# Shifting the start of the resident moving operands within their slots, by 16 to 256 bytes

## The chip, the cores and the metric

The kernel runs on one core of a Trainium2 chip. The metric is the device time of one execution, in microseconds. A profiled execution gives the trace; other executions are only timed.

## What is computed

One layer of a streaming encoder, on a prompt of 4096 rows and a sample of 32 rows, each row 1024 wide, in float32. The parts that matter here:

```
h = rmsnorm(x, norm_g)
proj = jnp.einsum('btd,de->bte', h, w_in)
u, v, z_a, xb, z_b = jnp.split(proj, [W_A, 2 * W_A, 3 * W_A, 3 * W_A + W_B], axis=-1)
v_n = layernorm(v, ln_v_g, ln_v_b)
a = u * chunk_mlp(v_n, w_spatial, b_spatial) * jax.nn.silu(z_a)
...
b = pool_mix(x_ext, pos0, w_pool, pool_scale) * jax.nn.silu(z_b)
y = x + jnp.einsum('bte,ed->btd', jnp.concatenate([a, b], axis=-1), w_out)
...
y_prompt = rmsnorm(xp, final_g)
```

`chunk_mlp` mixes the 128 positions of a chunk by a matrix per head; `pool_mix` takes trailing means of 2, 4, 8 or 16 rows, followed by a linear map per group of channels. Also returned are the last 15 rows of the pooling branch and the normalised v of the sample.

## The kernel before

**Products.** Each large product of two matrices is cut into 2 x 2 blocks and done with seven block products instead of eight (the operands are sums and differences of blocks, `q` from 0 to 6). Every float32 operand is split into a high and a low part of type float32r; a block product takes three terms (high x high, high x low, low x high) for each of four slices of the contraction: twelve matmuls, in `product` (line 186, the matmul is line 193) and in `OutPair.product` (line 708, matmuls on lines 712 to 714). A matmul has a stationary operand of 128 x 128 and a moving operand of 128 partitions by 512 columns in most places.

**Slots.** `slot()` (line 105) hands out one of seven buffers, one for each `q`, of 2 * 4 * 528 float32 (16896 bytes, 33 x 512) in each of the 128 partitions. In the program's memory layout they follow one another from byte 18432 (36 x 512) of a partition, so each begins at a multiple of 512 bytes. A slot holds a moving operand for a whole stage, while stationary operands (`weight_tile`, line 624, tiles named wop, also at multiples of 512 bytes) pass by. The stages:

- A first phase (lines 211 to 613) turns the normalised rows into operands and computes v, the slots holding v's weights (`wv`, line 264). It stores the operands of the rows in memory (`xops`, `xops_l`).
- Four blocks of 1024 rows each (`Tokens`, line 915). The slots hold the rows' operands, and the sixteen column sets of the input projection (`Set`, line 938: eight of kind gate, eight of kind pool) pass as stationary. Block 0's slots are filled by `load_first` (line 589): six of seven get two quarters by DMA and two by a VectorE and a ScalarE copy (lines 599, 600), the seventh comes by DMA alone. Blocks 1 and 2 are filled by `Tokens.load` (line 922, DMAs on line 931), block 3 by its other branch (line 926).
- The output projection in two halves z = 0 and 1 of the contraction. Here the slots hold operands made of `w_out`, loaded by `load_out_weights` (line 632, DMA on line 634), and the rows pass as stationary in sixteen pairs of 128 rows (`OutPair`, line 657; `LastPair`, line 746, is the last of all, and does its last product in two parts of 256 columns). Two small sample products use the same slots (`OutSample`, lines 843 to 845).

**Where a matmul starts in its slot.** `Tokens.moving` (line 933) gives it. In blocks 0 to 2 a slot is laid out as (half h, quarter j, slice k, 128 columns), and a matmul reads for one h and k the four quarters: four runs of 512 bytes, 2048 bytes apart, starting at h x 8192 + k x 512 bytes. In block 3, whose halves carry 16 sample rows each, the layout is (h, k, 528 columns), and a block product is done as two groups of 264 columns: one run of 1056 bytes, starting at h x 8448 + k x 2112 bytes, plus 1056 for the second group. The output weights are laid out as (k, h, 512 columns): one run of 2048 bytes.

**Order.** The order of the products is written out in lists (lines 1078 to 1091). At a change of stage two sets or pairs a and b run lagged: (a,0), (a,1), (b,0), (a,2), (b,1), (a,3), (b,2), (a,4), (a,5), (b,3), (a,6), (b,4), (b,5), (b,6). After b's product q the slot q is free, and its next contents are loaded by SP's queue (lines 1165 to 1171, 1266 and 1267). The next stage begins in the same lagged order, so its seventh slot is wanted ten products after the stage's first. On SP's queue the loads of the weights of the next sets and of the rows stand between the slot loads. While gate sets run, four spatial matmuls (line 998) stand between products at two places of each set.

Of the kernel before, what the change touches and what calls it, by code (L numbers as in the profile page):

```python
# [9 lines left out]
F32R = mybir.dt.float32r  # L10
# [5 lines left out]
P = 128  # L16
D = 1024
# [8 lines left out]
NB = 4  # L26
# [3 lines left out]
WIDE = HALF + EXT  # L30
TOT = SEQ + DEC
NQ = 7
WARM = 14


@with_exitstack
def stream_step(ctx: ExitStack, tc, x_prompt, x_sample, state_pool, norm_g, w_in, ln_v_g, ln_v_b,
# [18 lines left out]
    slots = ctx.enter_context(tc.tile_pool(name="slots", bufs=NQ))  # L56
# [45 lines left out]
        return y, guess + 3 * [lambda: stt(t, y, y, m, ALU.mult, ALU.mult),  # L102
                               lambda: stt(y, t, 1.5, y, ALU.add, ALU.mult)]

    def slot():
        return slots.tile([P, 2 * 4 * WIDE], F32R, tag="slot", name="slot")


    behind = []
# [101 lines left out]
    with ExitStack() as ph:  # L211
# [23 lines left out]
        def tr_tile():  # L235
            return ps_tr.tile([P, 512], F32, tag="tr", name="tr")

        g_bc = g_p.tile([P, D], F32, name="g_bc")
        first_ops = {}
# [9 lines left out]
        warm = tr_tile()  # L249
        for _ in range(WARM):  # L250
            tc.keep_in_program_order(nc.tensor.transpose(warm[:, :P], ident, ident))
# [10 lines left out]


        wv = [slot()[:, :8 * HALF].rearrange("p (h k n) -> p h k n", h=2, n=HALF) for _ in range(NQ)]

        v_raws = {}
# [87 lines left out]
        class Past:  # L354


            def load(self):
                self.st = half(), half()
                for z in range(2):
                    nc.gpsimd.memset(self.st[z][:HALO], 0.0)  # L360
                    nc.sync.dma_start(self.st[z][1:HALO], state_pool[0, 0, :, z * 512:(z + 1) * 512])
# [226 lines left out]

        def load_first(q):

            first_ops[q] = t = slot()
            dst = t[:, :8 * HALF].rearrange("p (h j x) -> p h j x", h=2, j=4)
            src = xops[0].rearrange("j p (q h x) -> q h p j x", q=NQ, h=2)
            n = 2 if q < NQ - 1 else 4
            for h in range(2):
                nc.sync.dma_start(dst[:, h, :n].bitcast(F32), src[q, h, :, :n])
            if n == 4:
                return
            nc.vector.tensor_copy(dst[:, :, pa.j], pa.ops[q])
            nc.scalar.copy(dst[:, :, pb.j], pb.ops[q])  # L600
# [4 lines left out]
        for n, (pair, q) in enumerate(lagged(pa, pb)):  # L605
            for step in {0: steps[:2], 1: steps[2:3], 2: steps[3:4], 4: steps[4:5], 6: steps[5:6], 7: steps[6:]}.get(n, []):
                step()
            if n == 1:
                norms([], [(v, P) for v in pairs[-3].v])
                pairs[-3].store()  # L610
            pair.product(q)
            if pair is pb:
                load_first(q)
# [16 lines left out]
    w_slots = {}  # L630

    def load_out_weights(z, q):
        w_slots[z, q] = t = slot()[:, :4 * D].rearrange("p (k h n) -> p k h n", k=4, h=2)
        nc.sync.dma_start(t.bitcast(F32), wops[z, q].rearrange("p k (h n) -> p k h n", h=2))

    class OutWeights:
# [227 lines left out]
    with ExitStack() as ph:  # L864
# [50 lines left out]
        class Tokens:  # L915
# [4 lines left out]
                self.groups = [(0, HALF)] if not self.last else [(0, WIDE // 2), (WIDE // 2, WIDE // 2)]  # L920

            def load(self, q):
                t = slot()
                self.ops[q] = t
                if self.last:
                    nc.sync.dma_start(t.bitcast(F32), xops_l[q].rearrange("p x t -> p (x t)"))
                    return
                src = xops[self.b].rearrange("j p (q h x) -> q h p j x", q=NQ, h=2)
                for h in range(2):
                    dst = t[:, h * 4 * HALF:(h + 1) * 4 * HALF].rearrange("p (j x) -> p j x", j=4)  # L930
                    nc.sync.dma_start(dst.bitcast(F32), src[q, h])
# [214 lines left out]
        for n in range(n_sets):  # L1146
# [9 lines left out]
            for s, q in order:  # L1156
                at += 1
                prepare(at + LEAD)
                while later:
                    (later.pop(0) or (lambda: None))()  # L1160
                for c, c0, w in cs[id(s)]:
                    s.product(c, q, c0, w)
                if n == 0 and q == 0:
                    behind.append(s)
                if s is g[-1] and groups[n + 1][0].stage != s.stage:
                    if n + 1 < n_sets:
                        groups[n + 1][0].tok.load(q)
                    else:
                        if q == 3:
                            groups[n_sets][1].begin([raw_tile(), raw_tile()], True)  # L1170
                        load_out_weights(0, q)
                if n == 0 and s is g[-1] and q in (3, 5):
                    next(constants, None)
                if s.kind == "gate" and q in (2, 4):
                    if q == 2:
                        s.t1 = []
                    s.t1.append(s.spatial(len(s.t1)))
                if s.kind == "gate" and q == 6 and s.tok.last:
                    s.spatial_sample()
                if q == NQ - 1:  # L1180
                    later.append(s.finish_gate() if s.kind == "gate" else s.finish_pool())
# [4 lines left out]
    with ExitStack() as ph:  # L1186
# [56 lines left out]
        for n in range(n_sets, len(groups)):  # L1243
# [6 lines left out]
            for m, (s, q) in enumerate(order):  # L1250
                at += 1
                prepare(at + LEAD)
                if m == 0 and n in samples:
                    samples[n].load()
                k = n - n_sets - 4
                if k == KT and m == 2:
                    sample_rows()
                if 0 <= k < KT and m in (0, 2):
                    state_load(k) if m == 0 else state_split()
                s.multiply(q)  # L1260
                if n == n_sets and s is g[0] and q == NQ - 1:
                    s.finish()
                if m == 2 and ended:
                    for x in ended:
                        x.finish()
                if s is g[-1] and n + 1 < len(groups) and groups[n + 1][0].stage != s.stage:
                    load_out_weights(1, q)
                if 0 <= k < KT and m == 6:
                    state_rows(k)
# [34 lines left out]
```

## Time and profile before

| | us |
|---|---|
| median of 2 runs | 2347.69 (2346.55 to 2348.82) |
| span of the profiled execution | 2345.9 |
| TensorE busy | 2328.8 |
| VectorE busy | 1790.2 |
| ScalarE busy | 896.4 |
| GpSimd busy | 215.1 |

The span runs from the first to the last instruction of one profiled execution; the timed runs count a little around it. Busy time of an engine is the time in which it has an instruction under way. "PE" is TensorE's matmuls, "PEld" its weight loads, which run beside them; a matmul's busy time contains its latency, so neighbours overlap, and the distance from start to start is what one costs in a row of many.

### The profile page before, as it was taken

Reading aid. Unit: us, or ns where it says so; the run is one execution under the profiler, and the core shown is the slowest. Engines: PE = TensorE matmul, PEld = TensorE weight load, DVE = VectorE, ACT = ScalarE, POOL = GpSimd, SP = SyncE. Lnnn points to the kernel's source line nnn. Section 1 sums busy time; section 2 is a strip of 40 time slices with the busy share of each in tenths; the row PEclk is TensorE's granted clock in tenths of the full one; section 3 lists DMA queues with packets and bytes.
Section 4 is the critical chain, followed back from the end, with each engine's and each line's share of the span. In section 5 each row is a group of like instructions: output and inputs, shape, how many; then the busy total and the mean of one; then the engine's idle time right before and its main releaser. Section 6 shows DMA issues by size and latency. Waiting matters only on the chain.

```text
span 2345.9 us, 32604 instructions
## 1 busy us (share of the span) xinstructions
PE 2328.8 (99%) x11936; PEld 1981.3 (84%) x11936; DVE 1790.2 (76%) x3318; ACT 896.4 (38%) x1603; POOL 215.1 (9%) x398
## 2 busy tenths in 40 slices
PE   8999999999999999999999999999999999999998
PEld 7878888888888888888888899999987878888877
DVE  7877786866787767877668876668777778688887
ACT  6545544433433333433334333334322333233333
POOL 1010000100021000111000110102200000000000
PEclk9999999999999999999999999999999999999999
DMA  8879977432448334483334472335587776955542
GB/s 309 316 241 279 275 255 245 142 104 89 149 144 296 99 100 134 135 300 122 108 108 148 177 262 87 101 100 164 223 294 265 252 257 232 360 171 169 159 137 90
DMA packets 325145, 445.69 MB, mean 190 GB/s; under 512 B 19324, under 2 KB 248444, under 8 KB 322296
## 3 DMA queue, kind: packets, MB, share of 16 engines
q1 hardware_dynamic: 273384, 355.05, 45.9%
q0 software_dynamic: 22288, 73.48, 8.3%
q10 hardware_dynamic: 29312, 15.08, 2.4%
q8 instruction: 94, 1.54, 0.3%
q14 instruction: 67, 0.55, 0.1%
HBM read 273.88 MB, written 169.66 MB: 189 GB/s over the span
## 4 chain that ended last, share of the span: by engine, by line
PE 95%; DMA 2%; DVE 2%; issue 0%; ACT 0%; SPq 0%; ACTq 0%; DVEq 0%
PE acc L193 66%; PE acc L712 8%; PE acc L713 8%; PE acc L714 8%; PE sp L998 2%; PE tr L473 1%; DMA wops<-raw 1%; DMA vt<-in_w_in_dram 1%; PE acc L261 0%; DMA op<-in_w_in_dram 0%; PE more L844 0%; PE more L843 0%; DVE wop L81 0%; DVE y L724 0%; PE acc L202 0%
## 5 line engine op out<-in xcount | busy, mean ns | idle before, releaser
L193 PE MATMUL acc<-slot,wop 128*128 128x512 f32 (+1 forms) x6720 | 1260.9, 348 | 1.0 <-DVE wop L81 1.0
L193 PEld LDWEIGHTS acc<-slot,wop 128*128 128x128 f32 x6720 | 1081.1, 188 | 156.5 <-DVE wop L81 1.4
L81 DVE TENSOR_TENSOR wop<-raw,wop 128x512 fp32r<-128x512 f32 (+1 forms) x510 | 353.4, 695 | 133.0 <-ACT wop L119 121.7
L119 ACT CAST wop<-raw 128x512 fp32r<-128x512 f32 x340 | 210.5, 622 | 384.4 <-PE acc L193 266.9
L712 PE MATMUL acc<-slot,wop 128*128 128x512 f32 x892 | 347.2, 389 | 1.5 <-DVE y L724 1.5
L713 PE MATMUL acc<-slot,wop 128*128 128x512 f32 x892 | 347.1, 389 | 0.0
L714 PE MATMUL acc<-slot,wop 128*128 128x512 f32 x892 | 347.0, 389 | 0.0
L193 PE MATMUL acc<-slot,op 128*128 128x512 f32 x1344 | 323.8, 395 | 0.3 <-ACT vt L167 0.2
L193 PEld LDWEIGHTS acc<-slot,op 128*128 128x128 f32 x1344 | 247.6, 188 | 51.9 <-ACT vt L167 0.7
L165 DVE TENSOR_TENSOR t<-acc,t 128x512 f32<-128x512 f32 (+1 forms) x320 | 186.7, 584 | 120.0 <-ACT t L174 65.5
L724 DVE TENSOR_TENSOR y<-acc,y 128x512 f32<-128x512 f32 x235 | 159.3, 687 | 72.6 <-PE acc L714 72.2
L712 PEld LDWEIGHTS acc<-slot,wop 128*128 128x128 f32 x892 | 167.4, 188 | 37.8 <-ACT wop L677 2.3
L714 PEld LDWEIGHTS acc<-slot,wop 128*128 128x128 f32 x892 | 167.4, 188 | 34.8
L713 PEld LDWEIGHTS acc<-slot,wop 128*128 128x128 f32 x892 | 167.4, 188 | 34.7
L677 ACT CAST wop<-raw 128x512 fp32r<-128x512 f32 x160 | 98.7, 622 | 175.2 <-PE acc L714 164.9
L81 DVE TENSOR_TENSOR wop<-sum,wop 128x512 fp32r<-128x512 f32 x200 | 136.9, 685 | 25.7 <-ACT wop L119 24.9
L1017 POOL DMA_DIRECT2D abT<-t x128 | 69.2, 541 | 843.2 <-DVE t L1029 622.7
L119 ACT CAST wop<-sum 128x512 fp32r<-128x512 f32 x136 | 84.5, 622 | 96.9 <-PE acc L193 72.0
L1040 DVE TENSOR_TENSOR t<-t 128x527 f32<-128x527 f32 (+3 forms) x160 | 111.1, 698 | 0.6
L677 ACT CAST wop<-sum 128x512 fp32r<-128x512 f32 x64 | 39.7, 622 | 119.5 <-PE acc L714 96.3
L174 ACT COPY t<-acc 128x512 f32<-128x512 f32 (+1 forms) x80 | 40.2, 504 | 107.1 <-PE acc L193 105.4
L115 DVE TENSOR_TENSOR sum<-raw 128x512 f32<-128x512 f32 x68 | 46.8, 688 | 44.7 <-DMA raw<-in_w_in_dram 44.1
(236 smaller groups left out, 1955.0 us busy)
## 6 DMA issues: line engine op xcount, KB each, us to landing
raw<-in_w_in_dram SPq DMA_DIRECT2D x102, 512.0 KB, 4.3
xops<-op SPq DMA_DIRECT2D x72, 512.0 KB, 6.1
abT<-t POOLq DMA_DIRECT2D x128, 256.0 KB, 3.8
raw<-abT SPq DMA_DIRECT2D x64, 512.0 KB, 5.0
slot<-xops SPq DMA_DIRECT2D x30, 1024.0 KB, 9.6
slot<-wops SPq DMA_DIRECT2D x14, 2048.0 KB, 9.7
xt<-in_x_prompt_dram SPq DMA_DIRECT2D x32, 512.0 KB, 5.0
raw<-v_all SPq DMA_DIRECT2D x32, 512.0 KB, 3.3
```

What stands on the lines that cost most here:

```text
L81: return nc.vector.tensor_tensor(out, src, hi.bitcast(F32), ALU.subtract)
L119: pair = nc.scalar.copy(hi, src), lo_part(lo, src, hi)
L165: add = lambda o, x, y: nc.vector.tensor_tensor(o, x, y, ALU.add)
L193: mm(acc, stationary(s, k), moving(m, k), start=fresh and n == 0, stop=n == len(terms) - 1, skip_group_check=True)
L677: nc.scalar.copy(t[:, 0], src)
L712: mm(acc, x[:, 0, k, :], w[:, k, 0, c], start=fresh and k == 0, stop=False, skip_group_check=True)
L713: mm(acc, x[:, 0, k, :], w[:, k, 1, c], start=False, stop=False, skip_group_check=True)
L714: mm(acc, x[:, 1, k, :], w[:, k, 0, c], start=False, stop=k == 3, skip_group_check=True)
L724: nc.vector.tensor_tensor(y, self.acc[bank], y, ALU.add)
L998: mm(sp[:, a, :], self.v[:, 4 * hf + a, :], WT[:, h, :], start=True, stop=True)
L1017: nc.gpsimd.dma_start(abT[row, :, t0:t0 + HALF], t[:, :HALF])
L1040: tt(nxt[:, lo:HALO + m], s[:, lo:HALO + m], s[:, lo - step:HALO + m - step], ALU.add)
```

## The change

A slot's contents begin a given number of float32 past the slot's start: 8 (32 bytes) in block 0, 16 (64) in block 1, 32 (128) in block 2, none in block 3, 64 (256) for z = 0 and 4 (16) for z = 1 of the output projection. The buffers keep their size and place; the views into them, written by the loads and copies and read by the matmuls, are the same behind the shift. The 4096 float32 used and at most 64 in front fit into 4224. The first phase's `wv` calls `slot()` without a shift.

```diff
@@ -31,6 +31,7 @@
 TOT = SEQ + DEC
 NQ = 7
 WARM = 14
+SHIFT = (8, 16, 32, 0, 64, 4)
@@ -102,8 +103,9 @@
-    def slot():
-        return slots.tile([P, 2 * 4 * WIDE], F32R, tag="slot", name="slot")
+    def slot(shift=0):
+        t = slots.tile([P, 2 * 4 * WIDE], F32R, tag="slot", name="slot")
+        return t[:, shift:] if shift else t
@@ -588,7 +590,7 @@
         def load_first(q):
 
-            first_ops[q] = t = slot()
+            first_ops[q] = t = slot(SHIFT[0])
@@ -630,7 +632,7 @@
     def load_out_weights(z, q):
-        w_slots[z, q] = t = slot()[:, :4 * D].rearrange("p (k h n) -> p k h n", k=4, h=2)
+        w_slots[z, q] = t = slot(SHIFT[NB + z])[:, :4 * D].rearrange("p (k h n) -> p k h n", k=4, h=2)
         nc.sync.dma_start(t.bitcast(F32), wops[z, q].rearrange("p k (h n) -> p k h n", h=2))
@@ -920,7 +922,7 @@
             def load(self, q):
-                t = slot()
+                t = slot(SHIFT[self.b])
                 self.ops[q] = t
```

## The prediction

> **What bounds the kernel now.** I read the page first (busy time, slices, chain), then the chain of waits cut to single stages, then the timeline of the last output pair, then the DMA views.
>
> ```profile
> span 2345.9 us, 32604 instructions
> PE 2328.8 (99%) x11936; PEld 1981.3 (84%) x11936; DVE 1790.2 (76%) x3318; ACT 896.4 (38%) x1603; POOL 215.1 (9%) x398
> PEclk9999999999999999999999999999999999999999
> PE acc L193 66%; PE acc L712 8%; PE acc L713 8%; PE acc L714 8%; PE sp L998 2%; PE tr L473 1%; DMA wops<-raw 1%; DMA vt<-in_w_in_dram 1%; PE acc L261 0%; DMA op<-in_w_in_dram 0%; PE more L844 0%; PE more L843 0%; DVE wop L81 0%; DVE y L724 0%; PE acc L202 0%
> ```
>
> TensorE is busy 99% of the span at full granted clock, and the chain that sets the end is 66% line 193 plus three times 8% for lines 712 to 714: the products whose moving operand lies in the slots. So whatever these matmuls gain or lose each goes into the time in full, and what the other engines do goes in only if it arrives late. The matmuls that the change reaches:
>
> ```profile
> L193 PE MATMUL acc<-slot,wop 128*128 128x512 f32 x4032 | 928.1, 390 | 1.0 <-DVE wop L81 1.0
> L712 PE MATMUL acc<-slot,wop 128*128 128x512 f32 x892 | 347.2, 389 | 1.5 <-DVE y L724 1.5
> L713 PE MATMUL acc<-slot,wop 128*128 128x512 f32 x892 | 347.1, 389 | 0.0
> L714 PE MATMUL acc<-slot,wop 128*128 128x512 f32 x892 | 347.0, 389 | 0.0
> L193 PE MATMUL acc<-slot,wop 128*128 128x264 f32 x2688 | 332.9, 285 | 0.0
> L844 PE MATMUL more<-slot,wop 128*32 128x512 f32 x32 | 12.0, 394 | 0.0
> L843 PE MATMUL more<-slot,wop 128*64 128x512 f32 x28 | 10.9, 391 | 0.0
> L845 PE MATMUL more<-slot,wop 128*64 128x512 f32 x4 | 1.6, 394 | 0.0
> L713 PE MATMUL more<-slot,wop 128*128 128x256 f32 x8 | 2.3, 283 | 0.0
> ```
>
> Columns: count, then busy time and mean of one, then idle time before them. Shifted are the 4032 of blocks 0 to 2 (1344 each) and, in the output projection, 3 x 892 = 2676, the 64 sample matmuls (32 + 28 + 4) and 3 x 8 = 24 narrow ones: 2764. Together 6796. The 2688 with 264 columns are block 3, shift 0, untouched. The mean of one (390 ns) is latency of a pipelined instruction; the price is the spacing, which the chain gives as length of a piece by its count, and the windows give by stage:
>
> ```profile
> 397.08:720.64 323.56, 322.61 (x1487) 1.00 0.45 147
> 720.64:1039.84 319.20, 319.20 (x1474) 1.00 0.46 154
> 1039.84:1359.04 319.20, 319.20 (x1474) 1.00 0.46 154
> 1359.04:1704.40 345.36, 345.36 (x2834) 1.00 0.44 152
> 767.09 0.89 PE sp L998 x8
> 774.33 13.62 PE acc L193 x60
> 1409.61 5.83 PE acc L193 x48
> 1422.17 0.33 PE sp L1009 x2
> 1422.50 8.94 PE acc L193 x72
> 2324.68 0.39 PE L714 MATMUL acc<-slot,wop 128*128 128x512 f32 x1
> ...
> 2334.88 0.39 PE L714 MATMUL acc<-slot,wop 128*128 128x512 f32 x1
> 2335.11 0.28 PE L712 MATMUL more<-slot,wop 128*128 128x256 f32 x1
> ...
> 2337.86 0.28 PE L714 MATMUL more<-slot,wop 128*128 128x256 f32 x1
> ```
>
> The four windows are blocks 0 to 3, each from its first matmul to the first of the next stage (window, its length, TensorE busy); then pieces of the chain (start, length, count); then the timeline. Block 1: 16 spatial pieces (8 gate sets, two halves) of 0.89 us are 14.24; (319.20 - 14.24) / 1344 = 226.9 ns a matmul, and 13.62 / 60 = 227.0 agrees. Output projection: 45 steps from 2324.68 to 2334.88 are 226.7 ns for 512 columns; 23 steps from 2335.11 to 2337.86 are 119.6 ns for 256 columns. So a column costs (226.7 - 119.6) / 256 = 0.418 ns, and 226.7 - 512 x 0.418 = 12.5 ns are fixed per matmul. All of these start on multiples of 512 bytes.
>
> **The change, part by part.** Nothing is added or removed: same instructions, same sizes, same buffers and waits; only the start of slot contents moves.
>
> (1) The moving reads. Block 3 is the row of before that reads off the 512-byte grid: there a matmul starts at h x 8448 + k x 2112 + (0 or 1056) bytes into a slot, so at every multiple of 64, and for the second column group 32 past one. (345.36 - 14.24 - 8 x 0.33) / 2688 = 122.2 ns. The aligned rows give 12.5 + 264 x 0.418 = 122.9 ns. Off the grid costs nothing there. Ends: the chain's pieces of block 3 run from 5.83 / 48 = 121.5 ns (1.4 under the line) to 8.94 / 72 = 124.2 ns (1.3 over). I take 0, because the whole block is nearest to it; carried to 6796 matmuls the ends are -9.5 and +8.8 us. What block 3 does not show: a 16-byte start, and runs of 512 bytes that lie across the grid (its run is 1056 bytes in one piece). In blocks 0 to 2 a matmul reads four runs of 512 bytes, 2048 apart; the output weights are one run of 2048. Four runs cost 226.9, one 226.7: 0.2 / 3 = 0.07 ns for starting another run while all lie on the grid.
>
> The nearest rows therefore set the price of a start at under 0.1 ns, but aligned. [...]
>
> (2) The loads of the slots, issued by SP, write to shifted places.
>
> ```profile
> L931 SPq DMA_DIRECT2D slot<-xops x28: 359/500/3952, 690.9 to 1041.4; - x28
> DMA to landing us min/median/max: 5.6/9.6/15.9
> L634 SPq DMA_DIRECT2D slot<-wops x14: 319/330/457, 1672.6 to 2026.0; - x14
> DMA to landing us min/median/max: 8.5/9.7/15.5
> L596 SPq DMA_DIRECT2D slot<-xops x14: 359/420/934, 367.4 to 397.7; - x14
> DMA to landing us min/median/max: 3.8/5.4/12.5
> raw<-in_w_out_dram SPq DMA_DIRECT2D x8, 512.0 KB, 3.7
> spare<-in_w_out_dram SPq DMA_DIRECT2D x8, 512.0 KB, 4.8
> ```
>
> Each line of a load is followed by its time from issue to landing. Cover: the last L931 issue, 1041.4, is block 2's seventh slot. In the lagged order its first product is the eleventh of the block; the block starts at 1039.84, a product is 12 x 0.227 = 2.72 us, so it is wanted at 1067.0. At the longest landing it is there at 1057.3: 9.7 us spare. Likewise for the output weights: last issue 2026.0 + 15.5 = 2041.5, wanted ten products after the stage begins, which is when the last load is issued (it follows the old stage's last product in the program): 2026.0 + 27.2 = 2053, 11 us spare. Block 0: 397.7 + 12.5 = 410.2, wanted ten products after 397.08, at 424: 14 spare. The price: in the program's memory layout the spare tiles lie 480 bytes past a multiple of 512 and the raw tiles on one; the same source and size lands in 4.8 against 3.7 us, a factor of 1.3 at most from alignment. 15.9 x 1.3 = 20.7: 1062.1, before 1067.0. So 0, and the cover is gone at a factor of (1067.0 - 1041.4) / 15.9 = 1.61. Behind a slower load on SP's queue wait the raw loads of the next sets, which lead their use by several products too.
>
> [...]
>
> (3) Block 0's slots are partly written by copies on VectorE and ScalarE.
>
> ```profile
> L599 DVE CAST slot<-op x6: 684/690/694, 367.4 to 395.5; 128x1024 fp32r<-128x1024 f32 x6
> L600 ACT CAST slot<-op x6: 1049/1056/1062, 369.0 to 394.6; 128x1024 fp32r<-128x1024 f32 x6
> ```
>
> If the shifted target took VectorE's faster rate away, the nearest bound is ScalarE's rate for the same shape: 6 x (1.056 - 0.690) = 2.2 us of VectorE, spread over 28 us and with the same 14 us of cover as the loads beside them. If it got faster, nothing waits for it. So 0; uncovered, at most +2.2.
>
> Sum: 0 + 0 + 0. Profiled span 2345.9, median of the runs 2347.69, so 1.8 us lie around the span: 2347.7, say **2348**. The likeliest case's own range is 2348 - 9.5 - 0 to 2348 + 8.8 + 0: 2338 to 2357.
>
> **Rivals.** (B) Straddling runs stall the read (slower). Place: lines 193 and 712 to 714. Every 512-byte run that is off the grid touches one piece of SBUF more: 4 x 4032 + 2764 = 18892 starts. Price between 0.07 ns (the row above: +1.3 us) and a whole new stream, 12.5 ns: +236 us, 2584. It decides the sign past 2% (47 us) from 47 / 18892 = 2.5 ns a start. Where pieces are 64 bytes, only block 0 (5376) and the second output half (1382) pay: 6758 x 12.5 = 84 us, 2432. For it: no row has such runs. Against: block 3's 1056 bytes are not a whole number of 64-, 128- or 512-byte pieces, and its spacing still lies on the straight line by columns, so part pieces are free at least at the end of a run.
>
> (C) The fixed 12.5 ns come from the moving and stationary reads both beginning on the same grid (the wop tiles lie on multiples of 512), and the shift parts them (faster). All gone: 6796 x 12.5 = 85 us, 2263; over 2% from 6.9 ns. Against: in block 3 the two starts differ by 32 to 480 bytes in most matmuls, and 122.2 - 264 x 0.418 = 11.8 ns are still there.
>
> (D) The loads become late. Twice as long, block 2's last slot lands at 1041.4 + 31.8 = 1073.2, 6.2 us late; block 1 the same; each output half 2026.0 + 31.0 - 2053 = 4 us: about 21 us, 2369. For it: the 1.3 above; against: it needs 1.61 before anything shows.
>
> **How the numbers follow.** Forecast A (nothing moves) 0.76; B 0.13, of which 0.02 below 2.5 ns a start; C 0.07, of which 0.06 over 2%; D 0.04. The predicted time is A's. A alone holds 2338 to 2357. To leave out no more than 2 in 10 the range reaches up to D and the cheap end of B, 2372, and down to 2337. A measurement of this kernel can tell about 2% from no change, so: faster 0.06, same 0.76 + 0.02 + 0.01 + 0.04 = 0.83, slower 0.11.
>
> **What would show it.** A: blocks 0, 1, 2 again 323.6, 319.2 and 319.2 us long, output spacing 226.7 ns in both halves. B: longer blocks, each by its own shift: block 0 alone and the second output half with small pieces, all five stages with 512-byte ones; single matmuls spaced wider, no idle time. C: the shifted stages under 220 ns a matmul while block 3 stays at 122. D: spacing unchanged, TensorE idle before the first products of blocks 1 and 2 with a DMA into a slot as releaser. The forecast is wrong if any stage's spacing moves by over 1.5 ns, or if idle time appears at a stage's start.

## The result, and the profile after

| | us |
|---|---|
| before, median of 2 runs | 2347.69 (2346.55 to 2348.82) |
| after, median of 2 runs | 2374.94 (2374.70 to 2375.19) |
| ratio after / before | 1.0115 (1.0094 to 1.0135) |
| span of the profiled execution, before and after | 2345.9 and 2372.9 |

The change costs 27 us, 1.15%. Timed again beside two of the experiments on one chip it cost the same: 1.0111 (1.0096 to 1.0126).

The page of the kernel after, span, engines and granted clock:

```profile
span 2372.9 us, 32604 instructions
PE 2354.6 (99%) x11936; PEld 1981.4 (84%) x11936; DVE 1794.9 (76%) x3318; ACT 897.1 (38%) x1603; POOL 206.9 (9%) x398
PEclk9999999999999999999999999999999999999999
```

The same instructions, the same clock, TensorE busy 99% of a longer span: the time did not go into waiting. The windows of the kernel after, each from a stage's first matmul to the next stage's (blocks 0, 1, 2, 3, output halves 0 and 1; the last ends at the first of the 24 narrow matmuls):

```profile
396.25:728.24 331.99, 331.15 (x1487) 1.00 0.44 144
728.24:1050.39 322.15, 322.15 (x1474) 1.00 0.46 152
1050.39:1377.87 327.48, 327.48 (x1474) 1.00 0.45 152
1377.87:1722.82 344.95, 344.95 (x2833) 1.00 0.44 151
1722.82:2046.26 323.44, 319.96 (x1410) 1.00 0.78 270
2046.26:2362.23 315.97, 315.97 (x1366) 1.00 0.47 159
```

The prediction showed blocks 0 to 3 of the kernel before. The output halves of the kernel before, in the same view:

```profile
1704.24:2025.78 321.54, 320.02 (x1410) 1.00 0.79 272
2025.78:2335.11 309.33, 309.33 (x1365) 1.00 0.49 162
```

Stage by stage the difference is +8.4 us (shift 32), +2.9 (64), +8.3 (128), -0.2 (block 3, unshifted: 1359.04 to 1704.24 before), +1.9 (256) and +6.6 (16). With a first stage that ended 0.8 us earlier this makes 27.1; the spans differ by 27.0. The chain of the kernel after shows what became longer, one piece from each of blocks 0, 1 and 2 (start, length, count):

```profile
455.49 14.00 PE acc L195 x60
...
782.40 13.75 PE acc L195 x60
...
1105.32 13.99 PE acc L195 x60
```

Line 195 is line 193 of before. Sixty matmuls took 13.62 us there, now 14.00, 13.75 and 13.99: 233.3, 229.2 and 233.2 ns each in place of 227.0. The timeline of the last output pair, after (53 steps of 512 columns, then 23 of 256):

```profile
2349.72 0.39 PE L714 MATMUL acc<-slot,wop 128*128 128x512 f32 x1
...
2361.99 0.40 PE L716 MATMUL acc<-slot,wop 128*128 128x512 f32 x1
2362.23 0.28 PE L714 MATMUL more<-slot,wop 128*128 128x256 f32 x1
...
2364.84 0.28 PE L716 MATMUL more<-slot,wop 128*128 128x256 f32 x1
```

The wide ones went from 226.7 to 231.5 ns, and the narrow ones from 119.6 to 113.5: with the same 16-byte shift the wide matmuls became slower and the narrow ones faster. From here on, "spacing" is the mean distance from start to start within a stage, worked out from all its matmuls in the trace, without the distances over 300 ns, which hold a spatial piece or a wait. For the kernel after: 233.3, 229.0, 233.1 in blocks 0 to 2, 122.3 in block 3, 226.7 and 231.7 in the output halves; before: 226.9, 226.8, 226.8, 122.4, 226.8, 226.7.

The half with shift 256 has its old spacing; its 1.9 us are waits for VectorE inside that half, which the kernel before had too. They show in the groups by line of the kernel after (last: idle time and what ended it; 1.5 us before, and 2.8 in a second profile of the kernel after):

```profile
L714 PE MATMUL acc<-slot,wop 128*128 128x512 f32 x892 | 349.5, 392 | 3.5 <-DVE y L726 3.5
```

The loads and copies of the slots, after:

```profile
L933 SPq DMA_DIRECT2D slot<-xops x28: 360/500/4133, 697.6 to 1053.7; - x28
DMA to landing us min/median/max: 6.1/9.9/16.2
L636 SPq DMA_DIRECT2D slot<-wops x14: 319/330/457, 1691.2 to 2046.5; - x14
DMA to landing us min/median/max: 8.5/9.5/14.8
L601 DVE CAST slot<-op x6: 684/690/694, 366.5 to 394.6; 128x1024 fp32r<-128x1024 f32 x6
```

The loads stand as before within a few per cent (medians of 9.9 against 9.6 and 9.5 against 9.7 us; 10.2 and 9.8 in the second profile), and the copy still takes 690 ns. The last load of block 2 lands by 1053.7 + 16.2 = 1069.9 at the latest and is wanted at 1050.39 + 120 x 0.233 = 1078.4.

### The profile page after: what moved, and what is told of

Read it like the earlier page. It is cut to its first block, busy times and chain, and to the rows that moved or that the text cites. A ratio compares the mean times of both kernels' runs of the same rounds, so it can differ in the third digit from the quotient of the medians.

```text
span 2372.9 us, 32604 instructions
## 1 busy us (share of the span) xinstructions
PE 2354.6 (99%) x11936; PEld 1981.4 (84%) x11936; DVE 1794.9 (76%) x3318; ACT 897.1 (38%) x1603; POOL 206.9 (9%) x398
## 4 chain that ended last, share of the span: by engine, by line
PE 90%; issue 5%; DMA 2%; DVE 2%; ACT 0%; POOL 0%; SPq 0%; POOLq 0%; DVEq 0%; ACTq 0%
PE acc L195 66%; PE acc L714 6%; PE acc L715 6%; PE acc L716 6%; PE sp L1000 2%; PE tr L475 1%; DMA vt<-in_w_in_dram 1%; DMA wops<-raw 1%; DMA op<-in_w_in_dram 0%; PE more L846 0%; PE more L845 0%; DMA part<-y 0%; POOL part L737 0%; DVE wop L82 0%; DVE y L726 0%
## 5 line engine op out<-in xcount | busy, mean ns | idle before, releaser
L195 PE MATMUL acc<-slot,wop 128*128 128x512 f32 (+1 forms) x6720 | 1280.4, 351 | 0.8 <-DVE wop L82 0.8
L167 DVE TENSOR_TENSOR vt<-acc,vt 128x512 f32<-128x512 f32 x64 | 44.0, 688 | 42.7 <-ACT vt L176 29.2
```

Source lines behind the costliest of these rows:

```text
L167: add = lambda o, x, y: nc.vector.tensor_tensor(o, x, y, ALU.add)
L195: mm(acc, stationary(s, k), moving(m, k), start=fresh and n == 0, stop=n == len(terms) - 1, skip_group_check=True)
```

## The experiments

Each kernel is the changed one with the edit shown; where a diff has several lines with names, each kernel takes the line with its own. Shifts in the edits are in float32; in the text, in bytes. The totals are of one execution each, but for both_128 (ten) and the repeat of the change (four).

**Does the cost belong to the start, to the runs, or to the stage?** Three kernels move other shifts into each stage.

```diff
-SHIFT = (8, 16, 32, 0, 64, 4)
+SHIFT = (64, 128, 4, 0, 8, 32)     # sweep_a
+SHIFT = (16, 32, 8, 0, 16, 128)    # sweep_b
+SHIFT = (96, 48, 24, 0, 4, 64)     # sweep_c
```

> Shifts of blocks 0, 1, 2: 256, 512, 16 bytes; output halves: 32, 128. In the changed kernel the spacing was 233.3 ns (32 bytes), 229.0 (64), 233.1 (128) in the blocks, 226.7 (256) and 231.7 (16) in the output halves, 226.8 unshifted. Theory 'start': a cost per matmul by the start of its moving operand alone, however many runs it has: block 0 226.8, block 1 226.8, block 2 231.7, first half 233.3, second half 233.1. Theory 'runs': a cost per run, four in a block and one in the output: first half 226.8 + 6.5/4 = 228.4, second half 226.8 + 6.3/4 = 228.4, block 2 at 226.8 + 4 x 4.9 = 246. Theory 'stage': the cost belongs to what else runs in the stage, and any shift meets it: block 0 233, block 1 229, block 2 233, first half 226.7, second half 231.7.

> Shifts of blocks 0, 1, 2: 64, 128, 32 bytes; output halves: 64, 512. 'Start': 229.0, 233.1, 233.3, 229.0, 226.8 ns. 'Runs': the blocks the same, first half 226.8 + 2.2/4 = 227.4, second half 226.8. 'Stage': 233, 229, 233, 226.7, 231.7.

> Shifts of blocks 0, 1, 2: 384, 192, 96 bytes; output halves: 16, 256. 'Start' with the cost set by the shift modulo 256: block 0 as 128 bytes, 233.1; block 1 as 64 from the other side, 229.0 or more; block 2 new; first half 231.7, second half 226.7. 'Start' with the cost set modulo 512: block 0 is free to differ from 233.1. 'Runs': first half 231.7 too, blocks over that. 'Stage': 233, 229, 233, 226.7, 231.7.

Measured spacings in ns (shift in bytes in front), blocks 0, 1, 2 and the two output halves:

| | block 0 | block 1 | block 2 | half 0 | half 1 | total, us |
|---|---|---|---|---|---|---|
| sweep_a | 256: 226.9 | 512: 226.8 | 16: 231.6 | 32: 233.3 | 128: 233.0 | 2367.8 |
| sweep_b | 64: 229.0 | 128: 232.4 | 32: 233.3 | 64: 228.9 | 512: 226.8 | 2367.2 |
| sweep_c | 384: 232.4 | 192: 233.3 | 96: 233.3 | 16: 231.7 | 256: 226.7 | 2379.3 |

Block 0's piece of the chain in sweep_a (shift 256) and then in sweep_b (64):

```profile
474.75 13.62 PE acc L195 x60
```

```profile
475.39 13.75 PE acc L195 x60
```

At 256 the piece has exactly the 13.62 us of the kernel before, though it is block 0, and at 64 it has the 13.75 that block 1 had in the changed kernel. So "stage" falls. The window of half 0 in sweep_a, with its one run at 32 bytes:

```profile
1709.15:2037.54 328.39, 328.39 (x1411) 1.00 0.77 267
```

TensorE is busy for 8.4 us more than the 320.02 of before, about what block 0 with four runs paid at 32 bytes: 233.3 ns a matmul, and not 228.4. So "runs" falls as well. "Start" holds, and multiples of 256 cost nothing (226.7 to 226.9 ns): 384 costs what 128 costs in sweep_b (232.4). (At 128 there are two values, 232.4 and 233.1. The matmuls settle into one of two rhythms: distances between 228 and 241 that repeat every seven or eight matmuls, or 229 and 238 by turns.)

**Start against what?** The stationary tiles are moved 128 bytes by a pad ahead of their pool, without any shift in the slots; then with shifts chosen so that the two theories part; then the pad is put behind the stationary tiles, as a control. In both_128 slots and stationary tiles move alike.

```diff
-SHIFT = (8, 16, 32, 0, 64, 4)
+SHIFT = (0, 0, 0, 0, 0, 0)         # stat_128, others_128
+SHIFT = (32, 48, 16, 0, 48, 36)    # both_mix
+SHIFT = (32, 32, 32, 0, 32, 32)    # both_128
+    pool("pad_p", 1).tile([P, 32], F32, name="pad")    # ahead of sum_p in others_128 instead
     op_p = pool("wop_p", 7)
```

> No shift in the slots; the stationary tiles (and the pools behind them) begin 128 bytes past a multiple of 512. If the cost comes from where the moving operand stands against the stationary one: all three blocks and both output halves near 233. If it comes from the moving operand's own place: 226.8 everywhere, total as before the change (2348 us).

> Stationary tiles (and the pools behind them) 128 bytes past the grid; shifts of blocks 0, 1, 2: 128, 192, 64 bytes, output halves 192, 144. If the difference moving minus stationary, modulo 256, sets the cost, the differences are 0, 64, -64 (192), 64, 16: spacing 226.8, 229.0, 233.3, 229.0, 231.7 ns. If the two operands' own places each cost something, all are over 232, as shift 128 with the stationary on the grid (232.4 to 233.1) and stationary 128 with no shift (232.4 to 233.0) were.

> No shift; only the pools behind the stationary tiles (sums, gate and pool temporaries, output rows) begin 128 bytes later, slots and stationary tiles on the grid. If the stationary tiles made stat_128 slow: 226.8 ns, total as before. If one of the other moved tiles did: 232 to 233 ns, about +36 us.

> Shift 128 bytes in all slots but block 3's, and the stationary tiles 128 bytes past the grid as well, so the difference is 0 everywhere but in block 3. If only the difference counts: 226.8 to 227.2 ns in blocks 0 to 2 and both output halves, total within 3 us of the kernel before. [...]

| | block 0 | block 1 | block 2 | half 0 | half 1 | total, us |
|---|---|---|---|---|---|---|
| stat_128 | 232.4 | 232.4 | 232.4 | 233.0 | 233.0 | 2385.8 |
| both_mix | 227.2 | 229.0 | 233.3 | 228.9 | 231.7 | 2369.0 |
| others_128 | 226.9 | 226.8 | 226.8 | 226.9 | 226.7 | 2348.4 |
| both_128 | 227.2 | 227.2 | 227.2 | 226.9 | 226.7 | 2350.5 |

The kernel before, beside them, took 2347.3 to 2349.5 us. One piece of the chain of block 0 in stat_128 and in others_128, then of blocks 0, 1 and 2 in both_mix, then of block 0 in both_128:

```profile
455.21 13.95 PE acc L195 x60
```

```profile
456.09 13.62 PE acc L195 x60
```

```profile
475.28 13.65 PE acc L195 x60
...
774.62 13.75 PE acc L195 x60
...
1097.74 14.00 PE acc L195 x60
```

```profile
475.07 13.65 PE acc L195 x60
```

With the slots where they were, moving the stationary tiles alone made the pieces 13.95 us long; moving everything behind them left 13.62. And in both_mix, with the stationary tiles 128 past the grid, a shift of 128 costs almost nothing, while 192 costs what 64 costs with them on the grid, and 64 what 192 costs. All five stages met the numbers of the difference within 0.4 ns. So, in these runs, for starts at multiples of 16 bytes, the cost is set by the start of the moving operand minus the start of the stationary one, modulo 256 bytes; the stationary tiles were tried at two places, 0 and 128. both_128 confirms it in the total: every slot but block 3's is off the grid, and it takes 1.0013 (1.0004 to 1.0023) of the kernel before, where the change cost 1.0111. Its 3.2 us, just over the 3 expected, are 0.5 to 1.0 us in each stage but the last. So a place off the grid may have a small price of its own, 0.4 ns a matmul in blocks 0 to 2 (227.2 against 226.8); where that comes from is not shown.

**Other differences.**

```diff
-SHIFT = (8, 16, 32, 0, 64, 4)
+SHIFT = (1, 2, 12, 0, 1, 2)        # sweep_d
+SHIFT = (56, 40, 60, 0, 28, 52)    # sweep_e
```

> Small shifts, stationary on the grid: blocks 4, 8, 48 bytes; output halves 4, 8. [...] With a cost that grows smoothly from 0 with the distance: 4 and 8 bytes between 226.8 and 231.7. 48 bytes lies between 32 (233.3) and 64 (229.0).

> Stationary on the grid; blocks 224, 160, 240 bytes, output halves 112, 208. If a shift and its negative cost alike, 224 is as 32 (233.3) and 240 as 16 (231.7), but 192 cost 233.3 where 64 cost 229.0, so this is expected to fail; then all five lie between 229 and 235. If some shift is better than none, one of them is under 226.8.

sweep_d: 4 bytes 240.2 (block 0) and 238.1 (half 0), 8 bytes 240.1 (block 1) and 232.2 (half 1), 48 bytes 233.3; total 2412.1. All four small starts cost more than 16 bytes do (231.6 to 231.7 ns), so a cost that grows smoothly from 0 falls. Four and eight bytes do not cost the same in the output halves, and there they cost less than in the blocks; that would fit a cost per run, but no experiment parts runs from stages at these starts. 48 bytes lies at the upper end of what was expected, as dear as 32. sweep_e: 224 bytes 233.3, 160 bytes 234.3, 240 bytes 236.6, 112 bytes 231.2, 208 bytes 234.7; total 2394.2. 240 lies above what was expected, and none lies under 226.8.

**Why block 3 did not show it.** Two kernels change the width of the matmuls: block 3 in groups of 396 and 132 columns; and blocks 0 to 2 in two groups of 256 columns.

```diff
-SHIFT = (8, 16, 32, 0, 64, 4)
+SHIFT = (0, 0, 0, 0, 0, 0)         # uneven
-self.groups = [(0, HALF)] if not self.last else [(0, WIDE // 2), (WIDE // 2, WIDE // 2)]
+self.groups = [(0, HALF)] if not self.last else [(0, 396), (396, 132)]
...
+SHIFT = (0, 8, 4, 0, 0, 0)         # narrow
+self.groups = [(0, HALF // 2), (HALF // 2, HALF // 2)] if not self.last else [(0, WIDE // 2), (WIDE // 2, WIDE // 2)]
-return self.ops[q][:, :8 * HALF].rearrange("p (h j k t) -> p h k j t", h=2, j=4, t=P)[:, h, k]
+return self.ops[q][:, :8 * HALF].rearrange("p (h j k t) -> p h k j t", h=2, j=4, t=P)[:, h, k, c0 // P:(c0 + n) // P]
```

> No shift; block 3 in column groups of 396 and 132 instead of 264 and 264, the same number of matmuls. The prediction's straight line (12.5 ns and 0.418 ns a column): 178 ns and 68 ns, block 3 as long as before (345 us). If a narrow matmul is held by something that does not depend on its columns (its weight load, say): 132 columns about 120 ns, 396 columns 178 to 185, block 3 at 345 + 1344 x (0.120 + 0.180 - 0.244) = 420 us. In the second case block 3 could not show in the kernel before what a start costs.

> Blocks 0 to 2 with every product in two groups of 256 columns (twice the matmuls, starts as in the wide form), shifts of blocks 0, 1, 2: 0, 32, 16 bytes; output halves unshifted. The 24 narrow matmuls of the last pair took 119.7 ns unshifted and 113.7 at 16 bytes. If narrow matmuls do not show the cost of a difference: block 0 about 119.7, block 1 at most 120, block 2 114 to 117. If the cost per matmul is that of the wide ones: 119.7, 126.2, 124.5. Then block 3 (264 columns) should have shown it in the kernel before.

Block 3 of uneven in the windows, and 48 matmuls (24 of each width) in its chain:

```profile
1358.64:1772.88 414.24, 412.23 (x2834) 1.00 0.38 128
```

```profile
1456.52 6.98 PE acc L195 x48
```

One wide and one narrow matmul together take 6.98 / 24 = 290.8 ns; the straight line said 178.2 + 67.7 = 245.9. Twelve wide ones and twelve narrow ones follow each other by turns. By the single starts the wide ones take 177 to 185 ns, near the line, and the narrow ones 109 to 114 ns, but for the first of each twelve (mostly 235 ns wide, 62 narrow): in a row, a narrow matmul costs far more than its columns. Block 3 took 414 us, near the 420 expected for that case; the whole kernel took 2416.8. And 120 matmuls of 256 columns in narrow, in blocks 0, 1 and 2 (shifts 0, 32, 16):

```profile
464.78 14.39 PE acc L195 x120
...
801.17 14.00 PE acc L195 x120
...
1131.24 14.00 PE acc L195 x120
```

That is 119.9 ns unshifted, 116.7 at 32 bytes and 116.7 at 16 bytes: off the grid, narrow matmuls are 3 ns faster, where wide ones are 5 to 6 ns slower (total 2391.4 us). So matmuls of 132 columns are held by something other than their columns, and a difference in starts moves matmuls of 256 columns the other way. That block 3's own 264 columns behave like the 256 is carried over from the neighbouring width: no run gave all matmuls of block 3 one single difference.

**The change once more**, unaltered:

> The changed kernel unaltered, timed beside the two above on one chip: 27 us over the kernel before, with 233.3, 229.0, 233.1, 226.7 and 231.7 ns again.

Spacings 233.3, 229.0, 233.1, 226.8 and 231.7; median 2373.3 us against 2347.3.

## Why the prediction came out wrong

The measured 2374.9 us lie above the stated range of 2337 to 2372, and four of the five shifted stages moved by more than the 1.5 ns that I had named as the sign of being wrong.

**The bound** was read rightly: what the matmuls of the slots gain or lose each went into the time in full. Blocks 0 to 2 and half 1 gave 8.4 + 2.9 + 8.3 + 6.6 = 26.2 of the 27 us by spacing alone, with no new wait.

**Step (1) failed**, at "Off the grid costs nothing there", where I took 0 from block 3. Two things in it were wrong. The straight line through 256 and 512 columns took 119.6 ns at 256 columns for a fixed part and columns; uneven shows that narrow matmuls do not lie on it (109 to 114 ns at 132 columns, not 67.7). So that block 3 lay on the line said nothing about the wide ones. And narrow shows that at 256 columns the effect has the other sign: if 264 columns behave alike, block 3 could not have given even the sign for 512. The row was also a mixture of many differences. Measured, the terms that I set at 0 are +6.4, +2.2, +6.3, 0 and +5.0 ns a matmul, times 1344 each for the blocks and some 1340 for an output half. My upper end of 1.3 ns was up to five times too small.

**The price of a start** of under 0.1 ns was an estimate from rows on the grid. Off it, with the stationary tiles on it, shifts of 16, 32, 64 and 128 bytes cost 5.0, 6.4, 2.2 and 6.3 ns. Starts at 4 and 8 bytes took 240 ns in the blocks, more than any multiple of 16 that was tried (at most 236.6); but in half 1 a start at 8 bytes took 232.2 ns, less than the 233.3 of 32 bytes.

**Rival B** had the sign and the kind of trace (longer blocks, each by its own shift, no idle time), but not the mechanism: not the runs that lie across a grid, since one run paid as much as four (233.3 ns at 32 bytes in both) and a start of 256, which is off a 512-byte grid, paid nothing (226.7). That it had the sign was luck. **Rival C** had the quantity that decides, the start of the moving operand against that of the stationary one, but supposed that equal starts are the bad case. At 512 columns they are the best of the fifteen differences tried (226.7 to 227.2 ns; the next, 64 bytes, 228.9).

**Steps (2) and (3)** held: the medians of the slot loads moved little (9.6 us to 9.9, and 10.2 in the second profile; 9.7 to 9.5 and 9.8; block 0's 5.4 to 5.5 and 6.0), VectorE's copies kept 690 ns, and no matmul waited for a slot. **Rival D** did not occur.

## What to carry to other kernels

Where float32r matmuls of 512 columns bound a kernel, the starts of the moving and the stationary operands should be chosen together: here equal starts modulo 256 bytes were the best (226.7 to 227.2 ns), and a pad of 128 bytes ahead of one of the two pools cost 1.6% (stat_128, 2385.8 against 2347.6 us) without touching an instruction. A row priced at another width or over a mixture can mislead even in sign; before it is carried over, one has to know what holds it. An edit that uses another value in each stage reads like five experiments in one trace, provided the stages are compared each with itself.

## What the runs showed of the hardware that was not expected

The spacing of matmuls with 128 x 128 float32r weights and 512 columns, by the difference of the starts (moving minus stationary, modulo 256 bytes):

| bytes | 0 | 4 | 8 | 16 | 32 | 48 | 64 | 96 |
|---|---|---|---|---|---|---|---|---|
| ns | 226.7 to 227.2 | 238.1 to 240.2 | 232.2 to 240.1 | 231.6 to 231.7 | 233.3 | 233.3 | 228.9 to 229.0 | 233.3 |

| bytes | 112 | 128 | 160 | 192 | 208 | 224 | 240 |
|---|---|---|---|---|---|---|---|
| ns | 231.2 | 232.4 to 233.1 | 234.3 | 233.3 | 234.7 | 233.3 | 236.6 |

In the timeline of the kernel after, a weight load begins with the matmul ahead of the one that it is for:

```profile
1948.97 0.39 PE L714 MATMUL acc<-slot,wop 128*128 128x512 f32 x1
1948.97 0.19 PEld L715 LDWEIGHTS acc<-slot,wop 128*128 128x128 f32 x1
1949.20 0.39 PE L715 MATMUL acc<-slot,wop 128*128 128x512 f32 x1
1949.20 0.19 PEld L716 LDWEIGHTS acc<-slot,wop 128*128 128x128 f32 x1
```

So the load of the next weights runs beside the matmul, and one may suppose that the two reads get in each other's way when their places differ. The weight loads themselves did not become longer: their median is 188 ns before and after. The dependence on the difference of the two starts (226.7 to 240.2 ns) does not fit with two reads that are fully independent. That the two reads collide is an inference, though: no run took the weight load away or moved only the next one. Open also are why the period is 256 bytes, why 64 is cheaper than its neighbours, and why narrow matmuls gain.
